# Every fourth weight chunk's low part: ScalarE's negated high part plus an accumulating transfer, in place of VectorE's subtraction

## The chip, the cores and the metric

The program runs on one core of one Trainium2 chip. The metric is the device time of one execution in microseconds (us). The core has five engines with a queue of instructions each: TensorE (PE, with its weight loads as PEld), VectorE (DVE), ScalarE (ACT), GpSimd (POOL) and SyncE (SP). Transfers are issued from SP's and POOL's queues and are carried out by the core's 16 DMA engines.

## What is computed

A two-layer decoder trunk on 256 positions of width 2048, all in float32. Cut to what matters:

```python
def reference(x, p, w_in_a, ..., w_ple_gate, w_ple_proj):
    for i in range(DEPTH):                       # DEPTH = 2
        j = i // N_MIXERS
        if i % N_MIXERS == 0:
            y = sgu_mixer(x, w_in_a[j], ...)     # gelu/silu of x @ w_in (2048 x 6144), spatial mixing
        else:
            y = moba_mixer(x, w_in_b[j])         # attention, x @ w_in (2048 x 8192)
        y = y @ w_out[i]
        x = layer_norm(DEEPNORM_ALPHA * x + y, ln_g[i], ln_b[i])
        x = x + jax.nn.sigmoid(x @ w_ple_gate[i]) * (p[i] @ w_ple_proj[i])
    return x
```

Nearly all of the arithmetic is products of the 256 positions with weight matrices, about 190 MB of float32 weights that are read once.

## The kernel before, in words

A float32 product is made of three fast ones. Every operand is split into hi, the value rounded to the format `F32R`, and lo, the value minus hi; the product is x_hi·w_hi + x_lo·w_hi + x_hi·w_lo, one matmul on each of the lines 204, 206 and 208, accumulated in the same PSUM bank.

The weights are read in 180 chunks of 128 x 2048 (1 MB), in the order in which they are used: 16 for v, 16 for u and 16 for z of layer 0 (chunks 0 to 47), 16 for w_out, 2 for w_proj, 16 for w_gate, then for layer 1 16 for v, 32 for q and k, 16 for z, and again 16, 2 and 16. A chunk has its three steps in `load_weights` (line 110): it is loaded in two halves (the first three chunks in quarters) into buffers `wr`, of which there are four, by DMAs on SP's queue (line 120); ScalarE rounds each half into `wh` (line 121); VectorE subtracts `wh` from `wr` into `wl` (line 122). `wh` and `wl` have three buffers each, so a chunk's `wh` can only be written when TensorE has read the chunk three before it. `weights` (line 125) asks for chunks two ahead of the one in use. `row_unit` (line 182) is the use of one chunk: 24 matmuls of 512 columns. The chunks of v in layer 0 hold one row block of 2048 columns: four hi matmuls, four with x_lo, four lo, and the same for the other 128 positions. Most others hold four blocks of 512 columns, used block by block with hi, x_lo and lo in turn; the last of four chunks of an output slice takes all four blocks for the first 128 positions and then for the others (`both`). So the lo of a chunk's second half is first read at the 9th matmul of 24 of such a last chunk, at the 11th of a v chunk, at the 15th of the other block chunks.

The engines run their own queues in order and wait for each other by semaphores; Tile's scheduler has put the instructions of each queue in order when the program is built. POOL's queue holds little: masks of the mixing matrices (line 271), two powers for the layer norms (line 402, and line 299 for layer 0's v), a small transfer that writes the norms' gains and biases to DRAM (line 172), and 24 transfers that read them back broadcast over the partitions (line 179, buffers `gb`).

Of the kernel before, what the change touches and what calls it, by code (L numbers as in the profile page):

```python
# [10 lines left out]
AF = mybir.ActivationFunctionType  # L11
ALU = mybir.AluOpType
# [23 lines left out]
def f32(ap):  # L36
    return ap.bitcast(F32)
# [3 lines left out]
def decoder_trunk(ctx: ExitStack, tc: tile.TileContext, xT, pT, wv_a, wu_a, wz_a, w_sT, b_s,  # L41
# [5 lines left out]
    nc = tc.nc  # L47
# [59 lines left out]
    ready = []  # L107
    taken = [0]

    def load_weights():  # L110
        pat, kw, src = chunks[len(ready)]
        hi = wpool.tile([P, D], F32R, name="wh", tag="wh")
        lo = wpool.tile([P, D], F32R, name="wl", tag="wl")
        parts = 4 if len(ready) < 3 else PARTS
        n = D // parts
        for i in range(parts):
            c = slice(i * n, (i + 1) * n)
            b = slice(i * 4 // parts, (i + 1) * 4 // parts)
            raw = wpool.tile([P, D // PARTS], F32, name="wr", tag="wr", bufs=4)[:, 0:n]
            nc.sync.dma_start(raw.rearrange("p (b e) -> p b e", b=4 // parts), src[:, b])  # L120
            nc.scalar.activation(hi[:, c], raw, AF.Copy)  # L121
            nc.vector.tensor_sub(lo[:, c], raw, f32(hi[:, c]))  # L122
        ready.append((pat, kw, hi, lo))

    def weights(ahead=AHEAD):
        while len(ready) < min(taken[0] + 1 + ahead, len(chunks)):
            load_weights()
        taken[0] += 1
        w, ready[taken[0] - 1] = ready[taken[0] - 1], None
        return w  # L130
# [116 lines left out]
    def load_x(k):  # L247
        raw = t2("xr")
        if k:
            nc.sync.dma_start(in2(raw), xT[:, k:k + 2, :])  # L250
            t = split(raw, "x")
            xs[k:k + 2] = [t[:, u] for u in range(2)]
            return
        t = t4("x").rearrange("p (k h s) -> p k h s", k=2, h=2)
        for i in range(2):
            c = raw[:, i * S:(i + 1) * S]
            nc.sync.dma_start(c, xT[:, i, :])
            nc.scalar.activation(t[:, i, 0, :], c, AF.Copy)
            nc.vector.tensor_sub(t[:, i, 1, :], c, f32(t[:, i, 0, :]))
            xs[i] = t[:, i]  # L260
            if i == 0:
                load_weights()
# [368 lines left out]
```

## Time and profile before

| | us |
|---|---|
| median of 3 runs (1070.04 to 1070.73) | 1070.65 |
| the profiled execution's own time | 1070.59 |
| its span, first to last instruction | 1068.9 |
| TensorE busy in it | 1057.5 |
| VectorE busy | 616.8 |
| ScalarE busy | 499.5 |
| GpSimd busy | 24.5 |

TensorE's busy time overlaps with itself where matmuls are pipelined: one of 512 columns is shown with 0.39 us, but they follow each other every 0.227 us, 24 of them in 5.44 us. The mean granted TensorE clock is 0.999 of full speed, that is the 2.4 GHz level throughout. The DMA engines were busy for some 57% of the span.

### The profile page before, as it was taken

Reading aid. Unit: us, or ns where it says so; the run is one execution under the profiler, and the core shown is the slowest. Engines: PE = TensorE matmul, PEld = TensorE weight load, DVE = VectorE, ACT = ScalarE, POOL = GpSimd, SP = SyncE. Lnnn points to the kernel's source line nnn. Section 1 sums busy time; section 2 is a strip of 40 time slices with the busy share of each in tenths; the row PEclk is TensorE's granted clock in tenths of the full one; section 3 lists DMA queues with packets and bytes.
Section 4 is the critical chain, followed back from the end, with each engine's and each line's share of the span. In section 5 each row is a group of like instructions: output and inputs, shape, how many; then the busy total and the mean of one; then the engine's idle time right before and its main releaser. Section 6 shows DMA issues by size and latency. Waiting matters only on the chain.

```text
span 1068.9 us, 12836 instructions
## 1 busy us (share of the span) xinstructions
PE 1057.5 (99%) x4944; PEld 878.1 (82%) x4944; DVE 616.8 (58%) x763; ACT 499.5 (47%) x659; POOL 24.5 (2%) x46
## 2 busy tenths in 40 slices
PE   8999999999999999999999999999999999999997
PEld 6888888888888878888888888888888888887886
DVE  5646774555555695564545465555566555668552
ACT  5545453545433455444434455454465443345442
POOL 1100110000000000000000000000000000000000
PEclk9999999999999999999999999999999999999999
DMA  7775795566555555555555554444646455555561
GB/s 259 269 257 183 247 299 185 184 204 199 188 184 191 194 169 186 189 182 181 196 197 194 198 160 158 158 158 158 197 158 197 166 199 195 192 184 170 198 204 40
DMA packets 97262, 203.86 MB, mean 191 GB/s; under 512 B 6912, under 2 KB 9232, under 8 KB 97200
## 3 DMA queue, kind: packets, MB, share of 16 engines
q1 hardware_dynamic: 95184, 196.63, 54.9%
q0 software_dynamic: 2016, 6.40, 2.3%
q8 instruction: 39, 0.64, 0.3%
q14 instruction: 23, 0.19, 0.1%
HBM read 200.86 MB, written 2.15 MB: 190 GB/s over the span
## 4 chain that ended last, share of the span: by engine, by line
PE 82%; issue 14%; DMA 2%; DVE 1%; ACT 0%; POOL 0%; SPq 0%; POOLq 0%; ACTq 0%; DVEq 0%
PE qk L204 5%; PE g L208 5%; PE qk L208 5%; PE qk L206 5%; PE g L206 5%; PE g L204 5%; PE y L206 5%; PE y L204 5%; PE y L208 5%; PE z L204 4%; PE z L206 4%; PE z L208 4%; PE u L206 3%; PE u L204 3%; PE u L208 3%
## 5 line engine op out<-in xcount | busy, mean ns | idle before, releaser
L122 DVE TENSOR_TENSOR wl<-wr,wh 128x1024 fp32r<-128x1024 f32 (+1 forms) x366 | 433.4, 1204 | 334.0 <-ACT wh L121 324.7
L121 ACT ACTIVATE wh<-wr 128x1024 fp32r<-128x1024 f32 (+1 forms) x366 | 372.2, 1041 | 466.4 <-PE y L206 152.6
L204 PE MATMUL g<-wh,xn 128*128 128x512 f32 x256 | 101.7, 397 | 0.0
L204 PE MATMUL z<-wh,x 128*128 128x512 f32 x256 | 101.4, 396 | 0.0
L204 PE MATMUL qk<-wh,x 128*128 128x512 f32 x256 | 101.3, 396 | 0.0
L204 PE MATMUL y<-wh,b 128*128 128x512 f32 x256 | 100.1, 391 | 0.0
L208 PE MATMUL g<-wl,xn 128*128 128x512 f32 x256 | 100.0, 391 | 0.0
L208 PE MATMUL qk<-wl,x 128*128 128x512 f32 x256 | 100.0, 391 | 0.0
L208 PE MATMUL z<-wl,x 128*128 128x512 f32 x256 | 100.0, 390 | 0.0
L206 PE MATMUL qk<-wh,x 128*128 128x512 f32 x256 | 99.9, 390 | 0.0
L206 PE MATMUL z<-wh,x 128*128 128x512 f32 x256 | 99.8, 390 | 0.0
L206 PE MATMUL g<-wh,xn 128*128 128x512 f32 x256 | 99.8, 390 | 0.0
L208 PE MATMUL y<-wl,b 128*128 128x512 f32 x256 | 99.7, 389 | 0.0
L206 PE MATMUL y<-wh,b 128*128 128x512 f32 x256 | 99.6, 389 | 0.0
L208 PEld LDWEIGHTS z<-wl,x 128*128 128x128 f32 x256 | 48.1, 188 | 10.2
L208 PEld LDWEIGHTS g<-wl,xn 128*128 128x128 f32 x256 | 48.0, 188 | 10.2
L208 PEld LDWEIGHTS qk<-wl,x 128*128 128x128 f32 x256 | 48.1, 188 | 10.2
L208 PEld LDWEIGHTS y<-wl,b 128*128 128x128 f32 x256 | 48.1, 188 | 10.1
L204 PEld LDWEIGHTS y<-wh,b 128*128 128x128 f32 x256 | 48.1, 188 | 9.9
L206 PEld LDWEIGHTS y<-wh,b 128*128 128x128 f32 x256 | 48.1, 188 | 9.7
L206 PEld LDWEIGHTS g<-wh,xn 128*128 128x128 f32 x256 | 48.2, 188 | 9.5
L206 PEld LDWEIGHTS qk<-wh,x 128*128 128x128 f32 x256 | 48.1, 188 | 9.4
(142 smaller groups left out, 1421.9 us busy)
## 6 DMA issues: line engine op xcount, KB each, us to landing
wr<-in_wqkz_b SPq DMA_DIRECT2D x96, 512.0 KB, 4.1
wr<-in_w_out SPq DMA_DIRECT2D x64, 512.0 KB, 4.1
wr<-in_w_gate SPq DMA_DIRECT2D x64, 512.0 KB, 4.1
wr<-in_wu_a SPq DMA_DIRECT2D x32, 512.0 KB, 4.3
wr<-in_wz_a SPq DMA_DIRECT2D x32, 512.0 KB, 4.1
wr<-in_wv_b SPq DMA_DIRECT2D x32, 512.0 KB, 3.9
wr<-in_wv_a SPq DMA_DIRECT2D x26, 512.0 KB, 5.3
gb<-vecs POOLq DMA_DIRECT2D x24, 256.0 KB, 5.9
```

The costliest lines, as they stand in the source:

```text
L121: nc.scalar.activation(hi[:, c], raw, AF.Copy)
L122: nc.vector.tensor_sub(lo[:, c], raw, f32(hi[:, c]))
L204: nc.tensor.matmul(o(n), xh, wh[i][n], start=first, stop=False)
L206: nc.tensor.matmul(o(n), xl, wh[i][n], start=False, stop=False)
L208: nc.tensor.matmul(o(n), xh, wl[i][n], start=False, stop=last)
```

## The change

The chunks with index 3, 7, 11, ... 179, 45 of 180, get their lo in another way. ScalarE, after hi, writes minus hi into `wl`; then a DMA on POOL's queue reads the same raw weights from DRAM a second time and adds them to what stands in `wl`. VectorE does nothing for these chunks. Each of them is done in two halves, so there are 90 such ScalarE instructions and 90 such transfers of 512 KB.

```diff
             nc.scalar.activation(hi[:, c], raw, AF.Copy)
-            nc.vector.tensor_sub(lo[:, c], raw, f32(hi[:, c]))
+            if len(ready) % 4 == 3:
+                nc.scalar.activation(lo[:, c], f32(hi[:, c]), AF.Copy, scale=-1.0)
+                nc.gpsimd.dma_start(lo[:, c].rearrange("p (b e) -> p b e", b=4 // parts), src[:, b],
+                                    accum_op=ALU.add)
+            else:
+                nc.vector.tensor_sub(lo[:, c], raw, f32(hi[:, c]))
```

The scheduler's order of the queues follows. First ScalarE's queue at the start of the program, where chunk 3 is made (`wh_202`; `x` and `ws` are splits of the input and of the mixing matrices, `wh_236` or `wh_238` is chunk 4). Before:

```order
L75 ACTIVATE x_351<-xr_349 128x2x256
L75 ACTIVATE ws_425<-wsr_422 128x4x128
L121 ACTIVATE wh_202<-wr_204 128x1024
L121 ACTIVATE wh_202<-wr_208 128x1024
L121 ACTIVATE wh_236<-wr_238 128x1024
L121 ACTIVATE wh_236<-wr_242 128x1024
```

Now, in the same place of the same queue:

```order
L75 ACTIVATE x_353<-xr_351 128x2x256
L75 ACTIVATE ws_429<-wsr_426 128x4x128
L121 ACTIVATE wh_202<-wr_204 128x1024
L123 ACTIVATE wl_203<-wh_202 128x1024
L121 ACTIVATE wh_202<-wr_209 128x1024
L123 ACTIVATE wl_203<-wh_202 128x1024
L121 ACTIVATE wh_238<-wr_240 128x1024
```

The two negations stand each behind its own half's hi, and so the second half's hi and all of chunk 4 stand behind them. For some later chunks both hi come first and then both negations.

Second, POOL's queue from the last of the mixing masks (line 271, now 276) into layer 0's u, with the power for v's norm (`vrs`), the gains' way out to DRAM (`vecs`) and back (`gb`). Before:

```order
L271 AFFINE_SELECT wsr_580<-wsr_580 128x512
L299 TENSOR_TENSOR vrs_790<-vrs_790,half_77 128x2
L172 DMA vecs_94<-tv_832 96x128
L179 DMA gb_836<-vecs_94 128x512 x2
L179 DMA gb_839<-vecs_94 128x512 x2
L179 DMA gb_842<-vecs_94 128x512 x2
L179 DMA gb_845<-vecs_94 128x512 x2
L179 DMA gb_2274<-vecs_94 128x512 x2
```

Now; `wl_357`, `wl_517` and `wl_671` are chunks 7, 11 and 15 of v, `wl_857` is chunk 19, the last of u's first slice:

```order
L276 AFFINE_SELECT wsr_586<-wsr_586 128x512
L124 DMA wl_357<-in_wv_a 128x1024 x2
L124 DMA wl_517<-in_wv_a 128x1024 x2
L124 DMA wl_671<-in_wv_a 128x1024 x2
L304 TENSOR_TENSOR vrs_798<-vrs_798,half_77 128x2
L177 DMA vecs_94<-tv_840 96x128
L124 DMA wl_857<-in_wu_a 128x2x512
L184 DMA gb_844<-vecs_94 128x512 x2
L184 DMA gb_847<-vecs_94 128x512 x2
L184 DMA gb_850<-vecs_94 128x512 x2
L184 DMA gb_853<-vecs_94 128x512 x2
L124 DMA wl_857<-in_wu_a 128x2x512
```

Chunk 3's two transfers stand ahead of this piece, between the second mask and the third. The two halves of chunk 19 stand on either side of eight `gb` transfers, and those wait for `vecs` to have landed. The `gb` transfers of the two later norms, which stood in the queue far ahead of their use, have moved behind the transfers of z (layer 0), and among those of z (layer 1).

## Rows read from the trace of the kernel before

**Rows 1.** The page: the span, and each engine's busy time, share and instructions.

```profile
span 1068.9 us, 12836 instructions
PE 1057.5 (99%) x4944; PEld 878.1 (82%) x4944; DVE 616.8 (58%) x763; ACT 499.5 (47%) x659; POOL 24.5 (2%) x46
```

**Rows 2.** Busy time by stretch: PE, PEld, DVE, ACT, POOL, clock, DMA share, GB/s.

```profile
0.00:27.00 27.00, 23.25 (x94) 17.75 (x95) 14.75 (x22) 15.64 (x24) 5.16 (x16) 1.00 0.79 259
27.00:96.00 69.00, 69.00 (x306) 57.12 (x306) 39.89 (x38) 35.01 (x40) 2.81 (x2) 1.00 0.73 248
...
283.00:371.00 88.00, 88.00 (x394) 72.83 (x393) 50.14 (x52) 34.33 (x38) 0.00 (x0) 1.00 0.56 192
```

**Rows 3.** All waits of PE: for whom, us in total, times, longest.

```profile
PE v L204 <- ACT wh L121: 2.1, 4, 0.7
PE warm L243 <- POOL ident masks.py:199: 1.6, 1, 1.6
PE to L476 <- DVE r L460: 1.4, 1, 1.4
PE tp L235 <- DVE r L304: 1.2, 2, 0.6
PE pt L542 <- DVE sm L536: 0.5, 1, 0.5
```

**Rows 4.** The page's costliest groups: busy us, mean ns of one | idle before, what ended it.

```profile
L122 DVE TENSOR_TENSOR wl<-wr,wh 128x1024 fp32r<-128x1024 f32 (+1 forms) x366 | 433.4, 1204 | 334.0 <-ACT wh L121 324.7
```

**Rows 5.** ScalarE in order of time in a plain stretch: start, us, instruction, idle before.

```profile
300.01 2.01 ACT L121 ACTIVATE wh<-wr 128x1024 fp32r<-128x1024 f32 x2 [3.43 <-PE y L206]
305.45 2.01 ACT L121 ACTIVATE wh<-wr 128x1024 fp32r<-128x1024 f32 x2 [3.43 <-PE y L206]
310.89 2.01 ACT L121 ACTIVATE wh<-wr 128x1024 fp32r<-128x1024 f32 x2 [3.43 <-PE y L206]
```

**Rows 6.** DMA queues and issues: packets, MB, share; count, KB each, us to landing.

```profile
q1 hardware_dynamic: 95184, 196.63, 54.9%
wr<-in_w_out SPq DMA_DIRECT2D x64, 512.0 KB, 4.1
wr<-in_wv_a SPq DMA_DIRECT2D x26, 512.0 KB, 5.3
```

**Rows 7.** Landing times of all raw loads (line 120), then of all `gb` transfers.

```profile
DMA to landing us min/median/max: 2.7/4.1/10.0
...
DMA to landing us min/median/max: 3.8/5.9/8.5
```

**Rows 8.** DMA issues between 17 and 40 us, then between 104 and 126 us.

```profile
wr<-in_wv_a SPq DMA_DIRECT2D x10, 512.0 KB, 6.2
...
wr<-in_wu_a SPq DMA_DIRECT2D x7, 512.0 KB, 5.5
```

**Rows 9.** ScalarE in order of time where chunk 3 and chunk 4 are made.

```profile
23.27 2.24 ACT L121 ACTIVATE wh<-wr 128x1024 fp32r<-128x1024 f32 x2 [0.88 <-DMA wr<-in_wv_a]
25.81 2.23 ACT L121 ACTIVATE wh<-wr 128x1024 fp32r<-128x1024 f32 x2 [0.30 <-DMA wr<-in_wv_a]
```

**Rows 10.** PE in order of time where chunk 3 is used.

```profile
25.56 0.73 PE L204 MATMUL v<-wh,x 128*128 128x512 f32 x2 [0.45 <-ACT wh L121]
26.12 1.09 PE L206 MATMUL v<-wh,x 128*128 128x512 f32 x4
27.05 1.07 PE L208 MATMUL v<-wl,x 128*128 128x512 f32 x4
```

**Rows 11.** POOL in order of time where chunk 19 is made.

```profile
103.00 0.57 POOL L172 DMA_DIRECT2D vecs<-tv  x1 [0.83 <-ACT tv L170]
108.51 4.32 POOL L179 DMA_DIRECT2D gb<-vecs  x8 [4.95 <-DMA vecs<-tv]
```

**Rows 12.** ScalarE in order of time where chunks 19 and 23 are made.

```profile
101.37 1.06 ACT L121 ACTIVATE wh<-wr 128x1024 fp32r<-128x1024 f32 x1 [2.33 <-PE u L206]
...
125.76 1.99 ACT L121 ACTIVATE wh<-wr 128x1024 fp32r<-128x1024 f32 x2
```

**Rows 13.** PE in order of time at the first matmul of chunk 19.

```profile
112.56 0.39 PE L204 MATMUL u<-wh,x 128*128 128x512 f32 x1
```

## The prediction

> **What bounds the kernel now.** I read the busy times first. TensorE is busy for 1057.5 of 1068.9 us [rows 1]. By stretches, it is busy for all of 27 to 96 us and of 283 to 371 us, while the DMA engines have 0.73 and 0.56 of those stretches and VectorE some 57% [rows 2]. So TensorE's stream of matmuls sets the time. Its waits say what could be had from VectorE: all of them come to 6.8 us, and those that end with a VectorE instruction to 1.4 + 1.2 + 0.5 = 3.1 us [rows 3]. None of these is for `wl`. Freeing VectorE from 90 of its subtractions, 1.2 us each [rows 4], is thus worth 3.1 us at the very most, and I take 0, since those waits are for chains of the norms and the softmax, not for a late turn.
>
> The question is how late a changed chunk's lo can come. In a plain stretch ScalarE starts hi at T, just as TensorE reads the last of the chunk three before, and does so every 5.44 us [rows 5]. TensorE takes up the chunk at T + 10.9. A half's lo is now ready after hi, the negation, the issue and the landing. I count the negation as one more instruction of the kind of hi, 1.0 us (2.01 for two, [rows 5]); same engine, same shape. Both hi and both negations then end at T + 4.0, the first half's negation at T + 2.0 or, where both hi go first, T + 3.0. At 5.44 / 24 = 0.227 us a matmul the deadlines are T + 11.4 for the first half (3rd matmul), and for the second T + 12.7 in a last-of-four chunk (9th), T + 13.2 in a v chunk (11th), T + 14.1 in other block chunks (15th). From the end of the negation that leaves at least **8.4 us for a first half, and 8.7, 9.2 and 10.1 for a second**. What a transfer needs from there to landing I call L.
>
> **The price of L.** No accumulating transfer stands in the trace. Its nearest rows: a raw load of the same 512 KB takes 4.1 us from issue to landing as a median, 5.3 in the v stage [rows 6], at least 2.7 [rows 7]; a `gb` transfer, on the same POOL queue but half the size, 3.8, 5.9 and 8.5 us as least, median and most [rows 7]. A raw load occupies the 16 engines for 0.549 x 1068.9 us / 375 (196.63 MB in pieces of 0.524 MB) = 1.56 us [rows 1, 6]. The accumulating one must also read the old `wl`; I count that as a second pass, another 1.56 us, so 3.12 us of the engines each, and L = raw load's landing + 1.56 for a first half. The second half follows 1.0 us later and waits for the first's 3.12: L + 2.1. Low end: 3.8 for either half (the quickest on that queue). High end: the landing doubles, 8.2, with the second half another 4.1 - 1.0 behind, 11.3.
>
> The Trainium skill ("Collectives: The Full Stack", section "The bandwidth ceiling: the fold count and why AG ≠ RS ≠ AR") says that a transfer that adds reads two sources and so runs at half the rate of a copy, 32.35 against 62.28 GB/s there. By that rule two accumulating halves would hold the engines for 6.2 us (an estimate), and the rival below in which the DMA engines become the bound, which needs more than 9.3, would not come about; this trace has no such transfer to agree or not.
>
> **Plain stretches: nothing.** L is 4.1 + 1.56 = 5.7 for a first half, 7.8 for a second, against 8.4 and 8.7 to 10.1. In the v stage 6.9 and 9.0 against 9.2 or more. In the attention stage and at the norms other work lies between the chunks, so the cover is longer. If L went up by 1 us the cover of the last-of-four chunks would be gone; each further us costs up to 1 us for each of the chunks concerned. ScalarE's extra 90 x 1.0 = 90 us go into its idle time (busy 499.5 of 1068.9, [rows 1]).
>
> **The start: chunk 3.** Here there is no lead. TensorE takes hi of chunk 3 as it is made and reads its lo at 27.05 [rows 10]. ScalarE starts hi at 23.27, 1.1 us an instruction [rows 9]; with the negations in between it goes hi 24.4, negation 25.4, hi 26.5, negation 27.5. The second hi comes 0.95 us later than now, which disappears in what follows: the transfers are issued from 25.4 and 27.5. A raw load issued in this stretch lands after 6.2 us [rows 8], so the first half after 7.8, at 33.2, the second 3.12 behind, at 36.3. TensorE, in order, stands for 36.3 - 27.05 = **9.3 us**, less by nothing: it was running without a gap from there on, and everything behind moves with it. Low end, L = 3.8: 31.3, 4.3 us. High end, L = 11.3: 38.8, 11.8 us. Chunk 4's hi moves from 25.81 to about 27.5, hidden by that stall.
>
> **Chunk 19.** POOL's queue now has its second half behind eight `gb` transfers, and the first of these waits for `vecs` to land until 108.51; eight issues take 4.32 us, so the second half is issued at 112.83 [rows 11], though ScalarE, which starts at 101.37 [rows 12], has its negation done by about 106. TensorE starts chunk 19 at 112.56 [rows 13] and, a last-of-four chunk, reads the second half's lo at 114.4. With the 5.5 us of raw loads there [rows 8] + 1.56 = 7.1 it lands at 119.9: **5.5 us** late. Low, L = 3.8: 2.2. High, 8.2: 6.6. Who waits for POOL otherwise: `gb` itself is not late, since its wait for `vecs` ends after chunk 19's first half is issued. Chunk 23's hi is delayed in ScalarE's queue by v's norm and starts only at 125.76 [rows 12]; its cover is some 2 us short without the stall at chunk 19, but those 5.5 us come first and push TensorE away from it. I count 0 there; 2.2 if that cover does not come.
>
> **Sum.** 1070.59 of the profiled execution + 9.3 + 5.5 = 1085.4; the median of the runs is 0.06 above, so **1085.5 us**.
>
> **Rivals.**
> *Quick landing.* POOL's transfers land at the least of `gb`, 3.8 us: 1070.6 + 4.3 + 2.2 = 1077.1. For it speaks that the queue is empty where they go; against it that twice the bytes are moved, and that at the start raw loads took 6.2 us. The Trainium skill ("DMA: Bandwidth & Descriptors", section "Anatomy of one DMA — SWDGE (gpsimd) path") gives 2.0 us plus bytes over 436 GB/s for such a transfer, an estimate of 3.2 us for 512 KB, near this rival; the `gb` rows, 5.9 us for half of that, do not agree with it. Chance 0.10.
> *Every chunk late.* Landing doubles: 11.3 us for a second half, since the raw loads of the next chunks share the engines just then. Then 15 last-of-four chunks (without 19) lose 11.3 - 8.7 = 2.6 us, three v chunks 2.1, 13 others outside attention 1.2: 39 + 6 + 16 = 61 us (the 12 in attention, with their longer cover, nothing; chunks 3 and 19 make up the 45), and with 11.8 and 6.6 the time is 1150. For it: the DMA share is already 0.56 to 0.73. Chance 0.25.
> *DMA becomes the engine that bounds.* Four chunks take TensorE 21.8 us; their eight raw loads hold the DMA engines for 12.5 us. Two accumulating halves may thus take 9.3 us, three raw loads' worth each. At four they make it 25.0 us, 3.2 more for each of 45 groups: 144 us, 1215 or above. Chance 0.13.
> *Not slower.* If chunk 3's second half landed as quickly as the quickest raw load of all, 2.7 us, the start would cost 27.5 + 2.7 - 27.05 = 3.2 us and chunk 19 1.1, and if a freer VectorE took all 3.1 us out of its chains the time would be 1071.8, within 0.2%. It decides at an L of about 3 us, with VectorE's gain in full. Chance 0.05.
>
> **How the numbers follow.** The forecast, with its ends of 1078 to 1110, has 0.47. A measurement of this kernel can tell about 0.2% (2.1 us) from no change. Range: from 1076, just under the quick landing, to 1200, beyond every chunk late; the DMA bound and the not-slower case, 0.18 together, are left out. All cases but the last are slower by over 0.2%, 0.95; of the last, 0.03 is within and 0.02 faster.
>
> **What would show it.** Right: in the profile after, one wait of TensorE at some 28 us of about 9 us that ends with a transfer into `wl`, one at about 124 us (114 plus the first) of about 5, and no wait for `wl` in the w_out or attention stages; VectorE some 90 x 1.2 = 108 us less busy, ScalarE some 90 more; the accumulating transfers landing at 6 to 9 us. Wrong: many waits of 1 to 3 us on line 213's `wl` (late everywhere), or DMA shares near 1 with TensorE thinned evenly (DMA bound), or landings under 4 us (quick).

## The result and the profile after

The changed kernel takes 1195.4 us (median of four runs, 1179.23 to 1199.98) against 1070.69 us for the kernel before beside it (1070.04 to 1070.91): the ratio is 1.112, with a 95% interval of 1.108 to 1.115. The prediction said 1085.5 us. Its sign and its range hold; its size does not: 125 us were lost where 15 were forecast. The execution in the profile is the longest of the four, 1199.98 us, and the ratio is that of the other three; the granted clock is 0.964 in this one and 0.976 in the shortest.

The page of the changed kernel first: span, busy times, the granted TensorE clock in 40 slices (tenths), POOL's DMA queue (packets, MB, share of the 16 engines), and the group of VectorE's subtractions.

```profile
span 1198.3 us, 13067 instructions
PE 1099.2 (92%) x4944; PEld 898.5 (75%) x4944; DVE 512.4 (43%) x673; ACT 583.9 (49%) x749; POOL 126.3 (11%) x136
PEclk9799799999899999999999999999999999999989
q0 software_dynamic: 24192, 53.59, 24.2%
L127 DVE TENSOR_TENSOR wl<-wr,wh 128x1024 fp32r<-128x1024 f32 (+1 forms) x276 | 325.1, 1197 | 388.0 <-ACT wh L121 386.4
```

Against [rows 1], the span is 129.4 us longer. Two things make that up. TensorE's idle time (span less busy) is 1198.3 - 1099.2 = 99.1 us where it was 11.4, so 88 us are waiting. And its busy time went from 1057.5 to 1099.2 us for the same 4944 matmuls: 42 us are matmuls that ran slower. The clock row shows where: in the slices marked 7 and 8 part of the time has the 1.2 GHz level. The trace's clock record has that level, 0.50 of full, for 87 us of this span, and for 2 us before. VectorE's group for `wl` fell from 433.4 [rows 4] to 325.1 us and brought nothing.

What TensorE waits for in the changed kernel (for whom, what ended it, us in total, times, longest):

```profile
PE y L213 <- DMA wl<-in_w_out: 20.3, 7, 3.9
PE g L213 <- DMA wl<-in_w_gate: 16.6, 6, 4.5
PE v L213 <- DMA wl<-in_wv_a: 11.3, 5, 7.5
PE qk L213 <- DMA wl<-in_wqkz_b: 10.3, 7, 2.7
PE z L213 <- DMA wl<-in_wz_a: 8.7, 3, 4.2
PE u L213 <- DMA wl<-in_wu_a: 6.7, 2, 4.4
```

None of these stood in [rows 3]. In these lines thirty waits, 74 us, end with an accumulating transfer: two of them are the start, one is chunk 19, and the other 27 lie in stretches that the prediction had counted at nothing. Chunk by chunk the trace has seven more stalls there (27, 59, 75, 91, 139, 143 and 163), which the view counts in smaller lines or under another releaser; their matmuls too start within 0.2 us of such a landing. In all, TensorE waits for more than 0.3 us at 32 of the 43 changed chunks outside the two places, 70 us together. With 9.5 us at the start and 3.8 + 4.4 at chunk 19 these make up the 88. One of the 32 is chunk 51 in the w_out stage. TensorE there in order of time (start, us, instruction, idle before and what ended it):

```profile
346.61 0.39 PE L209 MATMUL y<-wh,b 128*128 128x512 f32 x1
346.83 0.39 PE L211 MATMUL y<-wh,b 128*128 128x512 f32 x1
349.98 0.69 PE L213 MATMUL y<-wl,b 128*128 128x512 f32 x1 [2.76 <-DMA wl<-in_w_out]
350.47 0.63 PE L209 MATMUL y<-wh,b 128*128 128x512 f32 x1
...
353.46 0.41 PE L211 MATMUL y<-wh,b 128*128 128x512 f32 x1
```

And POOL's queue for the same chunk:

```profile
337.52 1.22 POOL L124 DMA_DIRECT2D wl<-in_w_out  x1 [15.98 <-ACT wl L123]
339.56 1.21 POOL L124 DMA_DIRECT2D wl<-in_w_out  x1 [0.81 <-ACT wl L123]
```

By the trace the first half landed at 346.5 and the second at 349.8. The matmul that waits is the first lo of the chunk, the 3rd of its 24, and it starts 0.14 us after the **second** half has landed. Behind the wait the matmuls follow each other every 0.43 us instead of 0.227 until 353.46: the lower clock, paid on top of the wait.

Landing times in the changed kernel: accumulating transfers of w_out (count, KB each, median us from issue to landing), then all transfers of line 124:

```profile
wl<-in_w_out POOLq DMA_DIRECT2D x16, 512.0 KB, 8.7
...
DMA to landing us min/median/max: 5.8/9.3/12.0
```

Taken transfer by transfer from the trace, the 45 first halves have a median of 7.9 us and the 45 second halves one of 10.0; the second lands some 3 us behind the first, where it was issued 1 us behind it.

### The profile page after: what moved, and what is told of

It reads as the page before. It is cut to its first block, busy times and chain, and to the rows that moved or that the text cites. A ratio compares the mean times of both kernels' runs of the same rounds, so it can differ in the third digit from the quotient of the medians.

```text
span 1198.3 us, 13067 instructions
## 1 busy us (share of the span) xinstructions
PE 1099.2 (92%) x4944; PEld 898.5 (75%) x4944; DVE 512.4 (43%) x673; ACT 583.9 (49%) x749; POOL 126.3 (11%) x136
## 3 DMA queue, kind: packets, MB, share of 16 engines
q0 software_dynamic: 24192, 53.59, 24.2%
## 4 chain that ended last, share of the span: by engine, by line
PE 59%; DMA 28%; issue 7%; ACT 4%; POOL 1%; DVE 0%; SPq 0%; ACTq 0%; POOLq 0%; DVEq 0%
DMA wl<-in_wqkz_b 6%; DMA wl<-in_w_gate 5%; DMA wl<-in_w_out 5%; PE y L213 5%; PE y L209 4%; PE y L211 4%; PE z L213 4%; PE g L213 4%; PE z L209 4%; PE z L211 4%; PE qk L213 4%; PE g L209 4%; PE g L211 4%; PE qk L209 3%; PE qk L211 3%
## 5 line engine op out<-in xcount | busy, mean ns | idle before, releaser
L127 DVE TENSOR_TENSOR wl<-wr,wh 128x1024 fp32r<-128x1024 f32 (+1 forms) x276 | 325.1, 1197 | 388.0 <-ACT wh L121 386.4
L213 PE MATMUL y<-wl,b 128*128 128x512 f32 x256 | 103.6, 405 | 21.7 <-DMA wl<-in_w_out 20.3
L213 PE MATMUL g<-wl,xn 128*128 128x512 f32 x256 | 104.5, 408 | 19.4 <-DMA wl<-in_w_gate 16.6
L209 PE MATMUL g<-wh,xn 128*128 128x512 f32 x256 | 104.9, 410 | 0.0
L209 PE MATMUL y<-wh,b 128*128 128x512 f32 x256 | 103.3, 404 | 0.0
L209 PE MATMUL z<-wh,x 128*128 128x512 f32 x256 | 103.1, 403 | 0.0
L211 PE MATMUL g<-wh,xn 128*128 128x512 f32 x256 | 102.9, 402 | 0.0
L211 PE MATMUL y<-wh,b 128*128 128x512 f32 x256 | 102.7, 401 | 0.0
L209 PE MATMUL qk<-wh,x 128*128 128x512 f32 x256 | 102.4, 400 | 0.0
L211 PE MATMUL z<-wh,x 128*128 128x512 f32 x256 | 101.4, 396 | 0.0
L211 PE MATMUL qk<-wh,x 128*128 128x512 f32 x256 | 101.2, 395 | 0.0
L123 ACT ACTIVATE wl<-wh 128x1024 fp32r<-128x1024 f32 x90 | 91.8, 1048 | 0.5
L213 PE MATMUL u<-wl,x 128*128 128x512 f32 x128 | 52.4, 411 | 11.5 <-DMA wl<-in_wu_a 6.7
L211 PEld LDWEIGHTS y<-wh,b 128*128 128x128 f32 x256 | 50.0, 195 | 10.6
```

What stands on the lines that cost most here:

```text
L123: nc.scalar.activation(lo[:, c], f32(hi[:, c]), AF.Copy, scale=-1.0)
L209: nc.tensor.matmul(o(n), xh, wh[i][n], start=first, stop=False)
L211: nc.tensor.matmul(o(n), xl, wh[i][n], start=False, stop=False)
L213: nc.tensor.matmul(o(n), xh, wl[i][n], start=False, stop=last)
```

## The experiments

My theory from this: the second half of a block chunk is due with the first (the layout, below), some 2 us earlier than I had counted, and it lands 2 us later than I had counted; the lower clock then adds half as much again. Rivals: the extra DMA traffic slows everything evenly; ScalarE's 90 instructions delay the hi of later chunks; the places at the start and at chunk 19 weigh more than they seem. Each experiment is an edit of the changed kernel (the last one is shown as an edit of the kernel before), and its ratio is to the kernel before, with a 95% interval. Waits are given as TensorE's idle time in the view.

### Without the transfers, and with a plain one

```diff
                 nc.scalar.activation(lo[:, c], f32(hi[:, c]), AF.Copy, scale=-1.0)
-                nc.gpsimd.dma_start(..., src[:, b], accum_op=ALU.add)
```

> The accumulating transfers are left out; minus hi stays in wl for the 45 chunks, so w_hi takes part twice and lo not at all: its time is that of ScalarE's part and of VectorE's relief alone. Cover theory (TensorE stands because the second half's transfer lands some 10 us after its issue while the first lo matmul of a block chunk, which reads both halves, comes 7.4 us after the second negation): 1068 to 1073 us, no wait for wl left. Rival ScalarE (its 90 more instructions hold up hi): still above 1100. VectorE's relief is worth at most 3 us by the waits of before.

Measured: 1070.82 us, ratio 1.0004 (0.9994 to 1.0013). ScalarE is as busy as in the changed kernel and VectorE as free:

```profile
PE 1057.0 (99%) x4944; PEld 878.5 (82%) x4944; DVE 511.6 (48%) x673; ACT 584.0 (55%) x749; POOL 23.4 (2%) x46
q0 software_dynamic: 2016, 6.40, 2.2%
```

So the 90 negations cost nothing and the 90 subtractions saved are worth nothing; the rival of ScalarE falls. All of the loss hangs on the transfers, and no version that keeps them can beat the kernel before by this relief.

```diff
-                nc.gpsimd.dma_start(..., src[:, b], accum_op=ALU.add)
+                nc.gpsimd.dma_start(..., src[:, b])
```

> The same transfers from DRAM on POOL's queue, but overwriting wl instead of adding (lo is then the raw weight). Cover theory with the second read of the old value as the cause of the late landing: a half holds the engines for about 1.55 us instead of 2.94, the second half lands some 2.8 us sooner, at about 7 us, and the stalls nearly vanish outside the start and chunk 19: 1080 to 1110 us. Rival DRAM (the weights read twice load the memory): as the changed kernel, 1180 to 1200.

Measured: 1090.96 us, ratio 1.0190 (1.0175 to 1.0205), as expected. From its page, its waits and its DMA issues:

```profile
q0 software_dynamic: 24192, 53.59, 16.5%
PE u L212 <- DMA wl<-in_wu_a: 4.7, 1, 4.7
PE v L212 <- DMA wl<-in_wv_a: 4.2, 2, 2.8
wl<-in_w_out POOLq DMA_DIRECT2D x16, 512.0 KB, 6.5
```

The same bytes from DRAM, on the same queue, behind the same negations, land after 6.5 us and are late only at the start and at chunk 19 (and by 0.8 us at chunk 155). The waits in the plain stretches belong to the accumulation. What it does to the engines can be read from the shares: (24.2% x 1198.3 - 2.2% x 1069.0) / 90 = 2.96 us of all 16 for an accumulating half, (16.5% x 1088.0 - 23.5) / 90 = 1.73 us for a plain one.

### The deadline: lo last

In the changed chunks the 16 matmuls with hi go first and the 8 with lo last; the transfers and ScalarE's work stay. The rest of the edit, left out here, lets `three` do its hi or its lo matmuls alone; a changed chunk with an `order` of its own (the last of four, or the last of v) loses that order.

```diff
-        if order:
+        if (taken[0] - 1) % 4 == 3:
+            for what in "hl":
+                for i in range(len(ks)):
+                    for m in range(NM):
+                        three(i, m, range(NN), what)
+        elif order:
```

> In a changed chunk TensorE takes the 16 matmuls with hi first and the 8 with lo last; transfers and ScalarE as in the changed kernel. The first lo matmul, which in a block chunk needs both halves, then comes 3.2 us later, the cover of the second half goes from 7.4 to 10.6 us, and a landing of 10 us fits. Deadline theory: the stalls outside the start and chunk 19 go nearly all, the two places lose some 3 us less each, 1085 to 1110 us. Rival that engine load or DRAM traffic as such slows the program: 1170 to 1200.

Measured: 1103.64 us, ratio 1.0304 (1.0288 to 1.0319), as expected of the deadline but for chunk 19, which was to lose some 3 us less and waits 9.0 us. Its queue, waits and landing:

```profile
q0 software_dynamic: 24192, 53.59, 26.3%
PE u L215 <- DMA wl<-in_wu_a: 9.0, 1, 9.0
PE v L215 <- DMA wl<-in_wv_a: 6.5, 2, 3.5
PE y L215 <- DMA wl<-in_w_out: 4.0, 3, 3.5
wl<-in_w_out POOLq DMA_DIRECT2D x16, 512.0 KB, 8.9
```

The transfers are the same, land no sooner (8.9 us against 8.7) and hold the engines as long; only the first use of lo is 14 matmuls, 3.2 us, later. That takes back 92 of the 125 us by the medians (87 by the ratios), 3 of them at the start. The rival of the DMA traffic falls with it: an even thinning by the load would have stayed. What is left is the start, chunk 19 and chunk 51, the first changed chunk of w_out.

### The two thin places

Chunks 3 and 19 get their lo from VectorE again, in the changed kernel and in the version with lo last.

```diff
-            if len(ready) % 4 == 3:
+            if len(ready) % 4 == 3 and len(ready) not in (3, 19):
```

> Chunks 3 and 19 go back to VectorE's subtraction, the other 43 stay changed. Theory that most of the loss is the same short stall at each block chunk: only the two places' own stalls go (10.1 us at chunk 3, 4.0 + 4.8 at chunk 19, and some 5 us at the lower clock behind them), 1165 to 1178 us. Rival that the start sets the rhythm of all that follows: 1070 to 1100.

Measured: 1185.99 us, ratio 1.1072 (1.1055 to 1.1089), a miss: it was to be 1165 to 1178, and by the intervals it is not clear of the changed kernel, though the two chunks' waits alone come to 18 us there. TensorE's two longest waits at the start of this version:

```profile
55.42 1.19 PE L213 MATMUL v<-wl,x 128*128 128x512 f32 x2 [6.95 <-DMA wl<-in_wv_a]
59.23 1.19 PE L213 MATMUL v<-wl,x 128*128 128x512 f32 x2 [2.63 <-DMA wl<-in_wv_a]
```

They are those of chunk 3, now at chunk 7. The stretch has no lead at all, so the next changed chunk pays in its place; after chunk 19 it is chunk 23, with 4.8 us at 154.

> The same, and chunks 3 and 19 left to VectorE. Deadline theory: 1071 to 1082 us, with no wait of TensorE for a transfer above 1 us. Rival (engine load): above 1120. A gain over the kernel before from a freer VectorE: below 1069.

Measured: 1097.77 us, ratio 1.0252 (1.0233 to 1.0271), again a miss: TensorE stands at chunk 7 for 3.7 + 2.6 us, at chunk 23 for 4.5, and at chunk 51 for 3.8 at 327. Taking single chunks out does not repair a stretch without lead.

At chunk 19 the prediction held that POOL's `gb` transfers are in time. The test gives layer 0's `gb` transfers to SP's queue:

```diff
-            nc.gpsimd.dma_start(t[:, j, :], v.partition_broadcast(P))
+            (nc.gpsimd if i else nc.sync).dma_start(t[:, j, :], v.partition_broadcast(P))
```

> The changed kernel, with layer 0's eight gain and bias transfers on SP's queue, so that on POOL's queue chunk 19's two halves follow each other. Queue theory for chunk 19: its second half lands some 10 us sooner and the two stalls there, 4.0 us for VectorE's lo behind v's norm and 4.8 us for the transfer, go to 3 us or less together; the other stalls stay: 1180 to 1192 us. Rival (the stalls there come from v's norm itself or from the stage's loads): 8 us or more still there.

In the changed kernel POOL, VectorE and TensorE stood there like this:

```profile
123.57 3.80 POOL L184 DMA_DIRECT2D gb<-vecs  x7 [3.09 <-DMA vecs<-tv]
130.64 1.23 POOL L124 DMA_DIRECT2D wl<-in_wu_a  x1 [0.41 <-issue]
...
130.11 0.75 DVE L308 SCALAR_TENSOR_TENSOR v<-v,vmv,gb 128x512 f32<-128x512 f32 x1 [11.89 <-DMA gb<-vecs]
130.78 2.35 DVE L127 TENSOR_TENSOR wl<-wr,wh 128x1024 fp32r<-128x1024 f32 x2
...
133.19 0.80 PE L213 MATMUL u<-wl,x 128*128 128x512 f32 x1 [3.81 <-DVE wl L127]
...
140.07 0.77 PE L213 MATMUL u<-wl,x 128*128 128x512 f32 x1 [4.38 <-DMA wl<-in_wu_a]
```

VectorE's norm of v waits 11.9 us for the first `gb` (8.0 before) and chunk 20's subtraction stands behind it, done at 133.1. In the kernel before that was in time, because chunk 20 was used after chunk 19. The built order of the changed kernel has put the first matmuls of chunk 20 (its lo is `wl_893`) between chunk 19's hi and its lo (`wl_857`), on TensorE's queue, and the two waits above end in that order:

```
L213 MATMUL u_973<-wl_893,x_104 128x512 [waits DVE_49]
...
L213 MATMUL u_801<-wl_857,x_594 128x512 [waits DMASW4_49,DMASW3_49]
```

So chunk 20's lo is asked for as the 7th matmul from chunk 19's first instead of the 27th, 20 x 0.227 = 4.5 us sooner, and TensorE loses 3.8 us to VectorE before it loses 4.4 to chunk 19's second half. With the `gb` transfers on SP's queue:

```profile
119.30 1.19 POOL L124 DMA_DIRECT2D wl<-in_wu_a  x1 [0.81 <-ACT wl L123]
```

The second half is issued 11 us sooner, the wait for VectorE is gone, and one of 4.2 us for the transfer is left; 8.2 became 4.2, so half of that place is POOL's order and half the landing, between what the theory and its rival had said. The whole kernel measured 1185.69 us, ratio 1.1031 (1.0978 to 1.1084); by the intervals a gain in time over the changed kernel is not shown.

> The same on top of the kernel with the lo matmuls last, where one stall of 9.2 us is left at chunk 19. Queue theory: that stall goes to 3 us or less, 1090 to 1098 us. Rival: still 9 us there, 1101 to 1106.

Together with lo last it gave 1103.88 us, ratio 1.0310 (1.0295 to 1.0325), no better than lo last alone and a miss of the 1090 to 1098 us. The wait itself went as the theory had it: the 9.0 us at chunk 19 went down to 0.6 + 0.8. But the stall moved on once more, and chunk 23 now cost 5.9 us. The hi of its second half waited for its raw load:

```profile
143.30 1.06 ACT L121 ACTIVATE wh<-wr 128x1024 fp32r<-128x1024 f32 x1 [1.30 <-DMA wr<-in_wu_a]
```

And its second accumulating transfer landed 12.4 us after its issue (10.1 with lo last alone). What made both late is not shown.

### The clock: fill the waits

In 19 chunks that stalled, nine matmuls with zeros stand ahead of the first lo matmul. They add nothing to the sums and 19 x 9 x 0.227 = 39 us to TensorE's work.

```diff
+            if i == 0 and m == 0 and taken[0] - 1 in FILL:
+                for _ in range(9):
+                    nc.tensor.matmul(o(0), zero, wh[0][0], start=False, stop=False)
             for n in ns:
                 nc.tensor.matmul(o(n), xh, wl[i][n], start=False, stop=last)
```

> The changed kernel with nine matmuls of a zero operand (2.0 us, they add nothing to the sums) put ahead of the first lo matmul of 19 changed chunks at which TensorE stood for about 2 us or more. They fill the stall, so the transfers are waited for as before, but TensorE works meanwhile. Theory that the lower clock behind a stall is a second price of the stall, paid for standing idle: the granted clock comes back to about 0.99 outside the start and chunk 19, and the time falls by 15 to 30 us, to 1165 to 1180. Rival that the clock falls for another reason (the added transfers' load): unchanged, 1180 to 1200, and clock 0.96 to 0.98.

Measured: 1176.37 us, ratio 1.0993 (1.0953 to 1.1032), 19 us less than the changed kernel by the medians and 13 by the ratios, with 39 us more work. Its page, and TensorE at chunk 51:

```profile
span 1176.5 us, 13410 instructions
PE 1116.6 (95%) x5115; PEld 914.2 (78%) x5115; DVE 512.5 (44%) x673; ACT 583.9 (50%) x750; POOL 126.1 (11%) x136
...
343.78 2.26 PE L217 MATMUL y<-wh,zero 128*128 128x512 f32 x9
346.60 0.47 PE L219 MATMUL y<-wl,b 128*128 128x512 f32 x1 [0.56 <-DMA wl<-in_w_out]
346.91 0.39 PE L212 MATMUL y<-wh,b 128*128 128x512 f32 x1
```

The stall is as long as it was, 2.26 us of zeros and 0.56 of waiting against a wait of 2.76, and behind it the matmuls keep full speed. Over the span: idle and zeros come to 59.9 + 38.8 = 98.7 us (99.1 in the changed kernel), while the busy time less the zeros is 1077.8 us against 1099.2. So the 21 us between the two profiles are the clock's alone, and the lower clock is a price of standing idle, not a property of the transfers. The mean granted clock bears it out in the other executions too: 0.964 to 0.976 in the four of the changed kernel, 0.984 to 0.987 in the four of this one. The start and chunk 19 were not filled and kept their lower clock; among the 19 filled chunks it is left behind two, 47 and 55, where TensorE still stood for 2.0 and 2.1 us after the zeros.

One chunk by itself proves nothing, for not every stall brings the clock down. In the changed kernel, chunk 63 waits longer than chunk 51, and its matmuls go on every 0.23 us:

```profile
426.87 0.47 PE L213 MATMUL y<-wl,b 128*128 128x512 f32 x1 [3.10 <-DMA wl<-in_w_out]
...
427.41 0.40 PE L211 MATMUL y<-wh,b 128*128 128x512 f32 x1
427.64 0.39 PE L213 MATMUL y<-wl,b 128*128 128x512 f32 x1
```

### What makes the landing late

The accumulating transfer takes the raw weights from `wr` in SBUF, not from DRAM:

```diff
-                nc.gpsimd.dma_start(..., src[:, b], accum_op=ALU.add)
+                nc.gpsimd.dma_start(lo[:, c], raw, accum_op=ALU.add)
```

> The accumulating transfer reads the raw weights from wr on chip instead of from DRAM again. Cover theory: still two reads and a write in the engines, landing at about 10 us, 1160 to 1200. Rival DRAM: the 47 MB read again are gone, 1075 to 1110.

Measured: 1110.16 us, ratio 1.0372 (1.0356 to 1.0387), some 50 us under the low end of what was expected and at the upper end of the rival's 1075 to 1110. Its queue share, landing and largest wait for a transfer (chunk 19):

```profile
q0 software_dynamic: 14976, 53.59, 25.7%
wl<-wr POOLq DMA_DIRECT2D x90, 512.0 KB, 5.6
PE u L212 <- DMA wl<-wr: 8.5, 1, 8.5
```

It holds the engines as long, (25.7% x 1109.8 - 23.5) / 90 = 2.91 us, yet it lands after 5.6 us (4.6 and 6.5 for the two halves), over 3 us sooner, and the plain stretches are free (0.3 us for a transfer, at chunk 155). So the landing is not set by the time on the engines alone; the source, or the 47 MB less that are read from DRAM, is part of it. The shape is not the cause: from SBUF each partition's piece goes in one run, but so it does in the nine flat chunks from DRAM, and those land after 7.8 and 10.0 us as the others do. Why a read from DRAM makes an accumulating transfer 3 us later than one from SBUF, while a plain one from DRAM takes 6.5, no run here tells.

The last experiment starts the transfer sooner: ScalarE writes minus hi from the raw weights ahead of hi, into a buffer of its own, and the other chunks keep two `wl` buffers of three. The last lines of the edit are left out.

```diff
-        lo = wpool.tile([P, D], F32R, name="wl", tag="wl")
+        lo = wpool.tile([P, D], F32R, name="wl", tag="wa" if added else "wl", bufs=1 if added else 2)
...
+            if added:
+                nc.scalar.activation(lo[:, c], raw, AF.Copy, scale=-1.0)
+                nc.gpsimd.dma_start(..., src[:, b], accum_op=ALU.add)
             nc.scalar.activation(hi[:, c], raw, AF.Copy)
```

> Minus hi is made from the raw weights, ahead of hi, into a wl buffer of the changed chunks' own, so that it need not wait for TensorE to free a buffer; the transfers are the same. The negations can start when the raw weights have landed, some 4 to 8 us sooner. Cover theory: the waits outside the start go, TensorE's clock stays at its upper level, 1075 to 1095. Rival DRAM or engine load: 1170 to 1200, since the same bytes move in the same time.

Measured: 1149.71 us, ratio 1.0739 (1.0721 to 1.0757), a miss. The waits for the transfers fell as expected (4.7 us in w_out, where it was 20.3), but others came, 12.7 us for the softmax (`sm`) alone:

```profile
PE pt L548 <- DVE sm L542: 12.7, 7, 5.7
PE y L214 <- DMA wl<-in_w_out: 4.7, 5, 2.4
```

A likely cause is the third `wl` buffer that the other chunks lost, with subtractions now waiting in VectorE's queue ahead of the softmax and the norms; it was not isolated, and the run decides nothing.

## Why the prediction was right or wrong

- **What bounds the kernel, and VectorE's relief: right.** TensorE's stream sets the time, and freeing VectorE is worth nothing: `e_neg_only` is equal to before within 0.2%. ScalarE's 84 us more went into its idle time, as said.
- **"Plain stretches: nothing": wrong, the term that failed.** The runs showed 70 us of waits there instead of none, and 42 us of slower matmuls behind the waits of the whole kernel. Three of its steps failed, as follows.
- **The deadlines in block chunks: wrong, the first step.** The prediction gave the second half 8.7 to 10.1 us, counting row blocks, as the description of the kernel before does (9th and 15th matmul). But in a block chunk the columns of a row block are spread over all four loaded blocks, so each lo matmul reads 128 columns of each and needs both halves. The built order of the changed kernel says it, at chunk 51's first lo matmul:

```
L213 MATMUL y_2212<-wl_2257,b_2253 128x512 [waits DMASW4_49,DMASW3_49,Activation_49]
```

  It waits for two transfers (DMASW); in the trace the wait there is for the semaphores of both of the chunk's transfers and ends with the second. Both halves are due at T + 11.4, and the second, with its negation done at T + 4.0, has a cover of 7.4 us. Chunks of v in layer 1, where the halves are waited for apart, have no wait at all at three of four chunks; and `e_lolast`, which moves this deadline by 3.2 us and leaves the transfers as they are, gives back 92 us. That is shown.
- **The landing L: too short by 2.2 us, the second.** The term was a raw load's 4.1 us on SP's queue plus 1.56, and 7.8 for a second half; measured 7.9 and 10.0. The 1.56 itself was right: an accumulating half holds the engines for 2.96 us, where the prediction had 3.12. The base was of the wrong queue: [rows 7] had 5.9 us for `gb` on POOL's, and `e_plain` measured 6.5 for 512 KB there; 5.9 + 1.56 + 2.1 = 9.6 would have been near. Either error alone would have left less (an estimate, without the clock): 7.8 against 7.4 is 0.4 us late, 10.0 against 8.7 to 10.1 at most 1.3. With both, 10.0 - 7.4 = 2.6 us are lost in a block chunk; chunk 51 lost 2.8.
- **The clock: not priced at all, the third.** 42 us of the 129 are matmuls at the 1.2 GHz level behind the waits; `e_fill` takes 21 of them back without touching a transfer. Taken together the late chunks cost their waits and about half as much again; chunk 63 paid for its wait alone.
- **The start: right at its place, its size in part by luck.** Forecast 9.3 us late at the second half; TensorE stood for 7.46 + 2.06 us:

```profile
34.36 1.22 PE L213 MATMUL v<-wl,x 128*128 128x512 f32 x2 [7.46 <-DMA wl<-in_wv_a]
37.64 1.19 PE L213 MATMUL v<-wl,x 128*128 128x512 f32 x2 [2.06 <-DMA wl<-in_wv_a]
38.63 1.91 PE L209 MATMUL v<-wh,x 128*128 128x512 f32 x4
```

  The four matmuls behind it take 1.91 us instead of 1.09 [rows 10]; this is the clock again. The luck: the halves landed 9.8 and 10.9 us after their issue, where 7.8 and 8.8 were counted, but were issued at 24.55 and 26.59, 0.9 us sooner than counted, and the forecast took the second half to be due with the first, two matmuls too early.
- **Chunk 19: right place, size 8.2 for 5.5 us.** The second half behind eight `gb` issues, as said, cost 4.4 us. The other 3.8 were not in the sum: `gb` reached the norm 2 us later than the shift of the whole explains (130.11 against 112.86 us, 17.3 later, where its issue is 15.1 later), and TensorE asked for chunk 20's lo 4.5 us sooner, which the built order would have told. Chunk 23 was counted at zero and lost 2.4.
- **The rivals.** Every chunk late (1150, 0.25) was the right one, by its mechanism and nearly by its size: its 61 us in plain stretches stand against 88 - 9.5 - 8.2 = 70 of idleness there (all, less the start and chunk 19). That nearness is luck in part: its landing of 11.3 was 1.3 us too long, as its deadline of the last-of-four chunks was 1.3 us too late. The rest is the clock. The DMA bound (1215) came nearer in time and is wrong: TensorE is not thinned evenly, and `e_lolast` runs the same transfers in 1103.6 us. The quick landing falls with the shortest landing, 5.8 us. Of the twelve chunks of attention counted at nothing, seven lost 0.4 to 2.7 us each, 13 us together (99 to 115, 139 and 143); the five between, which have the softmax work beside them, under 0.3.
- **The Trainium skill's two rules.** By the Trainium skill ("Collectives: The Full Stack", "The bandwidth ceiling: the fold count and why AG ≠ RS ≠ AR") a transfer that adds runs at half the rate. The traces come near it: 2.96 us of the engines against 1.73, 1.7 times as long. The estimate of 3.2 us for the landing of 512 KB on POOL's queue, from the Trainium skill ("DMA: Bandwidth & Descriptors", "Anatomy of one DMA — SWDGE (gpsimd) path"), does not agree: a plain one in `e_plain` took 6.5.

## What to carry to other kernels

Before a wait is costed, read from the built order which transfers the first consumer waits for: a layout that spreads each operand over the whole tile makes the last piece due with the first. Take a landing time from the queue that the transfer will use, under the load that it will meet, and price stalls of TensorE at more than their length where rows show a lower clock behind them. And where a stretch has no lead, taking one late piece out only hands its stall to the next; moving the first use later, as `e_lolast` did, is what gave time back.

## What the runs showed of the hardware beyond that

- TensorE's clock can fall behind short waits in a stream that is otherwise full, but does not behind each. Behind 2.76 us of idleness at chunk 51 the matmuls went at 0.43 us each from 349.98 to 353.46 (the 1.2 GHz level); behind 3.10 us at chunk 63 they went at 0.23. In all, 87 us of the changed kernel's span were at the lower level, and 35 with zero matmuls in 19 of the stalls.
- An accumulating transfer of 512 KB holds the 16 engines for 2.9 to 3.0 us whether its source is DRAM or SBUF, but lands after 9.3 us from DRAM and 5.6 from SBUF (medians of all 90).
- POOL takes 1.2 to 1.3 us to issue an accumulating transfer of a block chunk's half (medians of first and second halves) and 0.85 for a flat one; the plain one in `e_plain` takes 0.72 for a block chunk's half. These issues are what takes POOL's busy time from 24.5 to 126.3 us.
